# Layer 1's gate projection moved ahead of the attention loop and computed with seven half-size products

## The chip, the cores and the metric

One Trainium2 chip, one of its cores. The metric is device time in microseconds, median of several executions. TensorE is called PE, VectorE DVE, ScalarE ACT, GpSimd POOL, and SyncE SP; SP issues nearly all DMAs of this kernel, in order, from one queue.

## What is computed

Two layers over 640 tokens: 512 of a prompt and 8 x 16 of a sample group, 1024 features each. Layer 0 is a gated MLP with a spatial mixing per block of 128 tokens. Layer 1 is causal attention with 16 heads of 128 features and a learned forgetting bias; the sample group also reads 256 cached keys and values for each of its 8 rows. All is float32. The part that matters here, from the reference:

```
proj = h @ w_in
q, k, v = proj[..., :E], proj[..., E:2 * E], proj[..., 2 * E:3 * E]
z = proj[..., 3 * E:4 * E]
logf = log_sigmoid(proj[..., 4 * E:] + b_f)
...
op = (fox_attend_prompt(q, k, v, logf) * silu(z)) @ fox_w_out
```

h is 640 x 1024, and E is 2048, so that z is 640 x 2048. It meets the attention only at the very end, in a product element by element.

## The kernel before, in words

**Three products for one.** PE multiplies in a rounded float32 form. Each operand is kept as a high and a low part (`split`: ACT copies into the rounded form, DVE subtracts what was lost), and `mm3` (L249 to L251) issues three matmuls for each pair of operands.

**Weights.** `units` lists all weight panels in the order of use, 512 KB each. `fetch` issues the DMA of the next ones into three buffers `RAW`; `prefetch` splits them into the ring `W`, which has five slots of two halves (four in the attention part, where the fifth holds the split q and k of a head). `weights(n)` hands out the next n panels and asks `prefetch` to run ahead.

**Layer 0, seven products.** For u and z of each pair of 128-wide channel groups, `seven_products` (L523) does a 256 x 1024 by 1024 x 640 product as a 2 x 2 block product with seven half-size products in place of eight (Winograd's form of Strassen's scheme). A half-size product is 4 steps of 128 in depth, 128 channels by 320 tokens: 12 matmuls of 320 columns. It needs sums of weight blocks, which POOL makes for each pair (`left_operands`, L198, four operations), sums of blocks of h, which `right_operands` makes once (L400), and seven additions on DVE per pair to put the results together (L528, L538 to L543). z's end is a tanh on ACT (L582) and one operation on DVE (L583).

**Layer 1.** Heads go in eight pairs. `project_v`, `project_k`, `project_q` and `project_z` are generators that issue the matmuls of one pair with full depth, as `channel_steps` (L307) does for k, q and z: for a head 8 steps of 128 in depth, each with three matmuls of 384 and three of 256 columns, so 96 matmuls for a pair. `interleave` (L328) runs a generator and places pieces of other work between its steps, by a table of times. Lines 1090 to 1099 are the loop: first the projections of pair 0 alone, with the forgetting sums between them; then, for p = 0 to 6, the projections of pair p+1 with the attention of pair p in between, over a table of length 57 (p = 0 to 5: v, k, q and z) or 43 (p = 6: v, k and q alone). z of pair 7 runs after the loop, in `project_z(7)`. The attention of a pair is scores, softmax, transposes and values for two heads of the prompt (`prompt_pieces`) and two halves of the sample (`sample_pieces`); its cached keys come through one buffer in 8 DMAs of 128 KB (`load_k`, L974) with rows of 128 bytes, and are turned by DVE (`turn_k`, L992).

**Order.** A list scheduler sets the order of instructions on each engine's queue from the order of the code, the dependencies and its own model of time. The engines then run their queues in order.

Of the kernel before, what the change touches and what calls it, by code (L numbers as in the profile page):

```python
# [56 lines left out]
def hybrid_trunk(tc, x_prompt, x_sample, ck, cv, clf, p_prompt, p_sample, norm_pre, norm_post,  # L58
# [27 lines left out]
    c_sc = dram.tile([H, SEQ], F32, name="c_sc")  # L86
    cs_sc = dram.tile([P, 272], F32, name="cs_sc")
# [66 lines left out]
    for p in range(8):  # L154
        for part in (2, 1, 0, 3):
            for kk in range(2):
                u_rows(f_win[0], kk * 512, part * E + p * 256, 4, 256)
    u_tail(f_wout, 1)
# [3 lines left out]
    S0, S1 = 16, 48  # L162
    SEVEN = (0, 2)
    items = []
    for i in range(len(units)):
        if not S0 <= i < S1 or i % 4 - i % 2 not in SEVEN:
            items.append((i, None))
        elif i % 2 == 0:
            items += [(i, j) for j in range(4)]

    n0 = S1 + 16 + 2 + 8
    few = range(n0, n0 + 64 + 12)
    place, last_use = [], [-1] * (2 * NW)
    state = {"raw": 0, "used": 0}

    def raw_of(i):
        if S0 <= i < S1:
            z = (i - S0 + 1) % 4
            if z == NRAW:
                return r1(o_X, 1024)  # L180
        else:
            z = i % NRAW if i < S0 else (i + 1) % NRAW
        return RAW[:, z * 1024:z * 1024 + 1024]
# [7 lines left out]
    def left_operands(i, j):  # L191

        (a11, a21), (a12, a22) = ([raw_of(r).rearrange("p (k n) -> p k n", k=4)[:, :, z:z + P] for z in (0, P)] for r in (i, i + 1))
        s2, s3, s1, s4 = (SF[:, z * 512:z * 512 + 512].rearrange("p (k n) -> p k n", k=4) for z in range(4))
# [4 lines left out]
        return (a11, SF[:, :1024], SF[:, 1024:2048], raw_of(i + 1))[j]  # L199

    def prefetch(upto, i0=0):

        while len(place) < min(upto, len(items)):
# [15 lines left out]
            else:  # L219
                split(*((x.rearrange("p (k n) -> p k n", k=4) for x in (hi, lo)) if j == 0 else (hi, lo)), left_operands(u, j))  # L220
                if u > S0:
                    fetch(u + 4)
# [84 lines left out]
    def channel_steps(ws, hh, banks, splits=SPLITS):  # L307

        out = [bank(banks), bank(banks)]
        for k in range(8):  # L310
            w = [z[:, k % 4, hh * P:(hh + 1) * P] for z in ws[k // 4]]
            for (a, b), o in zip(splits, out):
                mm3(o[:, :b - a], w, h_at(k, a, b), k == 0, k == 7)
# [10 lines left out]

    def channel_unit(ws, hh, banks):
        return run(channel_steps(ws, hh, banks, ((0, TOK // 2), (TOK // 2, TOK))))
# [58 lines left out]
    o_X, o_ln, o_sum, o_th = 14208, 15232, 16256, 17216  # L385
# [4 lines left out]
    SF = pool2.tile([P, 2560], F32, name="sf")  # L390

# [6 lines left out]
    b11, b12, b21, b22, t_a, t_b = (r1(10240 + z * 1280, 1280).rearrange("p (k n) -> p k n", k=4) for z in (0, 1, 2, 3, 4, 0))  # L398

    def right_operands():  # L400

# [32 lines left out]
    for p in range(4):  # L434
# [4 lines left out]
        for kk in range(4):  # L439
# [5 lines left out]
            if (p, kk) == (1, 1):  # L445
                with queued("act", "dve"):
                    right_operands()
# [12 lines left out]
    fetch(S0 + 4)  # L460
# [25 lines left out]
    assert o_A + 256 <= o_X  # L486
# [31 lines left out]
    m1, u2, u3 = (r1(o_sum + z * HT, HT) for z in range(3))  # L518
    HALF = (slice(0, HT), slice(HT, TOK))

    UZ = (0, 1, 2, 3)

    def seven_products(into, done):  # L523

        rights = (quarter(0, 0), right_sum(1), quarter(0, 1), right_sum(0), quarter(1, 1), quarter(1, 0), right_sum(2))
# [24 lines left out]

    def eight_products(done):
        wz = weights(2)
        for i in range(2):
            for j, o in enumerate(channel_unit(wz, i, UZ)):
                done(i, j, o[:, :HT])
# [32 lines left out]
    for g in range(0, 16, 2):  # L588
        for part, finish in ((0, finish_u), (1, finish_z)):
            if 2 * part in SEVEN:  # L590
                seven_products(lambda i, j: uv_of(g + i)[part][:, HALF[j]], lambda i, j, c: finish(g, i, j, c))
            else:
# [552 lines left out]
```

## Time and profile before

| | us |
|---|---|
| median of 3 executions | 1334.62 (1334.31 to 1335.19) |
| profiled execution, its own time | 1334.83 |
| span of that execution | 1333.0 |
| PE busy | 1321.0 (99%) |
| DVE busy | 766.4 (57%) |
| ACT busy | 542.9 (41%) |
| POOL busy | 135.7 (10%) |

The time is that of the whole execution, the span reaches from the first to the last instruction of the program. Busy times of PE are a model of its pipeline: matmuls start before those ahead of them have ended, and the distance from one start to the next says what one of them costs. 172.87 MB go over the DMA queues in the span.

### The profile page before, as it was taken

How to read it: one execution, taken by the hardware profiler on the slowest of the kernel's cores; microseconds unless marked ns; L12 is line 12 of the kernel's file. 1: busy time of each engine (PE TensorE's matmuls, PEld its weight loads, DVE VectorE, ACT ScalarE, POOL GpSimd, SP SyncE). 2: the span in 40 equal slices, each digit the busy share in tenths (PEclk: the TensorE clock that was granted, in tenths of full speed). 3: DMA queues.
4: the chain of work that ended last, by engine and by line, in shares of the span. 5: the costliest groups of instructions: out<-in, count | busy, mean ns of one | idle time of the engine just before them, and what ended most of it. 6: DMA issues, size and time to landing. Idle time of an engine off the chain costs nothing.

```text
span 1333.0 us, 21550 instructions
## 1 busy us (share of the span) xinstructions
PE 1321.0 (99%) x8363; PEld 1191.6 (89%) x8363; DVE 766.4 (57%) x1581; ACT 542.9 (41%) x1025; POOL 135.7 (10%) x144
## 2 busy tenths in 40 slices
PE   9999999999999999999999999999999999999998
PEld 6888999999988788999999999999999998888786
DVE  7744899998844546544545454444545465544642
ACT  5434555444535334523433333433334344435341
POOL 1013444543000100000000000000000000000100
PEclk9999999999999999999999999999999999999999
DMA  6432334232324204688778575778778687243211
GB/s 224 138 100 70 120 114 130 66 109 68 127 95 158 78 18 127 178 142 158 138 154 176 145 163 141 164 144 163 125 151 169 152 212 235 101 149 111 64 64 47
DMA packets 299913, 172.87 MB, mean 130 GB/s; under 512 B 188769, under 2 KB 269201, under 8 KB 299810
## 3 DMA queue, kind: packets, MB, share of 16 engines
q1 hardware_dynamic: 299666, 171.23, 51.7%
q8 instruction: 65, 1.06, 0.3%
q14 instruction: 38, 0.31, 0.1%
q10 hardware_dynamic: 144, 0.26, 0.1%
HBM read 149.86 MB, written 21.59 MB: 129 GB/s over the span
## 4 chain that ended last, share of the span: by engine, by line
PE 94%; DVE 3%; issue 1%; ACT 1%; DMA 0%; POOL 0%; SPq 0%; DVEq 0%
PE pb L249 28%; PE pb L251 27%; PE pb L250 27%; PE pb L960 3%; PE pb L953 1%; PE pb L1014 1%; PE pb L1040 1%; PE pb L287 1%; DVE W L264 1%; PE pb L565 1%; PE pb L1037 1%; DVE R L583 0%; DMA RAW<-in_gmlp_w_in 0%; PE pb L1032 0%; DVE R L528 0%
## 5 line engine op out<-in xcount | busy, mean ns | idle before, releaser
L249 PE MATMUL pb<-A,W 128*128 128x384 f32 (+2 forms) x1024 | 330.2, 322 | 2.1 <-DVE R L538 1.8
L251 PE MATMUL pb<-A,W 128*128 128x384 f32 (+2 forms) x1024 | 317.1, 310 | 0.0
L250 PE MATMUL pb<-A,W 128*128 128x384 f32 (+2 forms) x1024 | 316.6, 309 | 0.0
L249 PE MATMUL pb<-W,A 128*128 128x512 f32 (+1 forms) x840 | 298.3, 355 | 2.1 <-ACT R L686 1.4
L251 PE MATMUL pb<-W,A 128*128 128x512 f32 (+1 forms) x840 | 293.7, 351 | 0.6 <-DVE A L264 0.6
L250 PE MATMUL pb<-W,A 128*128 128x512 f32 (+1 forms) x840 | 294.0, 350 | 0.0
L264 DVE TENSOR_TENSOR W<-RAW,W 128x1024 fp32r<-128x1024 f32 (+1 forms) x156 | 194.0, 1244 | 139.7 <-ACT W L263 137.5
L263 ACT ACTIVATE W<-RAW 128x1024 fp32r<-128x1024 f32 (+1 forms) x156 | 161.1, 1033 | 156.8 <-PE pb L250 65.1
L249 PEld LDWEIGHTS pb<-A,W 128*128 128x128 f32 x1024 | 193.0, 188 | 10.9 <-issue 6.8
L250 PEld LDWEIGHTS pb<-A,W 128*128 128x128 f32 x1024 | 193.0, 189 | 0.6
L251 PEld LDWEIGHTS pb<-A,W 128*128 128x128 f32 x1024 | 192.6, 188 | 0.4 <-issue 0.4
L249 PEld LDWEIGHTS pb<-W,A 128*128 128x128 f32 x840 | 159.1, 189 | 26.4 <-issue 3.1
L251 PEld LDWEIGHTS pb<-W,A 128*128 128x128 f32 x840 | 158.9, 189 | 21.1 <-DVE A L264 0.9
L250 PEld LDWEIGHTS pb<-W,A 128*128 128x128 f32 x840 | 159.0, 189 | 20.4 <-issue 0.4
L264 DVE TENSOR_TENSOR A<-R,A 128x640 fp32r<-128x640 f32 (+1 forms) x51 | 41.0, 835 | 74.1 <-ACT A L263 71.9
L992 DVE STREAM_TRANSPOSE r2b_t<-r2b_t 128x256 f32<-128x256 f32 x128 | 46.4, 413 | 33.9 <-PE pb L1014 26.2
L263 ACT ACTIVATE A<-R 128x640 fp32r<-128x640 f32 (+1 forms) x51 | 36.6, 746 | 67.7 <-PE pb L250 65.7
L249 PE MATMUL pb<-tb,W 128*128 128x320 f32 x192 | 59.8, 312 | 0.1
L251 PE MATMUL pb<-tb,W 128*128 128x320 f32 x192 | 59.5, 310 | 0.0
L250 PE MATMUL pb<-tb,W 128*128 128x320 f32 x192 | 59.5, 310 | 0.0
L273 POOL TENSOR_TENSOR SML<-SML 128x1 f32<-128x1 f32 x25 | 18.1, 724 | 385.1 <-DVE SML L271 380.5
L955 ACT ACTIVATE R<-pb 128x128 f32<-128x128 f32 (+1 forms) x64 | 27.9, 436 | 65.7 <-PE pb L953 65.4
(235 smaller groups left out, 1866.7 us busy)
## 6 DMA issues: line engine op xcount, KB each, us to landing
RAW<-in_fox_w_in SPq DMA_DIRECT2D x64, 512.0 KB
RAW<-in_gmlp_w_in SPq DMA_DIRECT2D x40, 512.0 KB
r2b_t<-in_cache_fox_v SPq DMA_DIRECT2D x32, 512.0 KB
r2b_t<-in_cache_fox_k SPq DMA_DIRECT2D x128, 128.0 KB
RAW<-in_gmlp_w_out SPq DMA_DIRECT2D x16, 512.0 KB
RAW<-in_ple_w_gate SPq DMA_DIRECT2D x16, 512.0 KB
RAW<-in_fox_w_out SPq DMA_DIRECT2D x16, 512.0 KB
out<-R SPq DMA_DIRECT2D x40, 128.0 KB
```

Of the source, the lines that this page charges most:

```text
L249: nc.tensor.matmul(out, lh, rh, start=start, stop=False)
L250: nc.tensor.matmul(out, lh, rl, start=False, stop=False)
L251: nc.tensor.matmul(out, ll, rh, start=False, stop=stop)
L263: nc.scalar.activation(out=hi, in_=src, func=AF.Copy)
L264: nc.vector.tensor_tensor(out=lo, in0=src, in1=f(hi), op=ALU.subtract)
L273: nc.gpsimd.tensor_tensor(out=q, in0=t, in1=mhalf, op=ALU.pow)
L287: nc.tensor.transpose(out=b[:, j * P:(j + 1) * P], in_=src[:, (4 * c + j) * P:(4 * c + j + 1) * P], identity=ident)
L565: nc.tensor.matmul(b0[:, t * P:(t + 1) * P], v_at(pnl, t)[:, c0:c0 + P], wm, start=True, stop=True)
L953: nc.tensor.transpose(out=tb[:, j * P:(j + 1) * P], in_=pr[:, j * P:(j + 1) * P], identity=ident)
L955: nc.scalar.activation(out=pt[:, :n], in_=tb[:, :n], func=AF.Copy)
L960: nc.tensor.matmul(O[:, d], v[:, j, hh * P:(hh + 1) * P], pt[:, j * P:(j + 1) * P], start=(j == 0), stop=(j == i))
L992: nc.vector.transpose(out=kt[:, hh, bl, :PAST], in_=kr[:, hh, bl])
```

## The change

z of pairs 0 to 6 is taken out of the projections of the loop. A stage of its own, between k of pair 0 and q of pair 0, computes it pair after pair with `seven_products`, and writes it to a DRAM tensor `z_sc` (640 KB a pair). In the loop, `z_again` reads it back at the start of each pair's attention. The order of the weight panels follows. All of p = 0 to 6 now use the table of length 43; p = 0 has later times for its sample pieces, since its cached keys are loaded at the loop's start. z of pair 7 stays where it was, after the loop.

What goes with it: `right_operands` is called a second time, for layer 1's h, and gives four sums (before, the fourth overwrote a quarter of h). The second large pool of SBUF holds these sums during the stage, and becomes the attention's buffers after it; the small tensors of the forgetting bias move to the first pool. POOL's four sums for each pair go to a part of that pool too, and `RAW` has a fourth slot in the stage.

The diff, cut to its core:

```
+    z_sc = dram.tile([H, P, TOK], F32, name="z_sc")
...
-    for p in range(8):
-        for part in (2, 1, 0, 3):
+    def u_pair(p, parts):
+        for part in parts:
             for kk in range(2):
                 u_rows(f_win[0], kk * 512, part * E + p * 256, 4, 256)
+
+    u_pair(0, (2, 1))
+    Z0 = len(units)
+    for p in range(7):
+        u_pair(p, (3,))
+    Z1 = len(units)
+    u_pair(0, (0,))
+    for p in range(1, 8):
+        u_pair(p, (2, 1, 0) if p < 7 else (2, 1, 0, 3))
...
+    SEVEN = ((16, 48, 14208), (Z0, Z1, 13504))
...
-    few = range(n0, n0 + 64 + 12)
+    few = range(Z1, n1 + 12)
...
-        for o, a, b, dst in ((t_a, b12, b11, 0), (t_b, b22, t_a, 1), (b21, b21, t_b, 2), (b12, b22, b12, None)):
+        for o, a, b, dst in ((b11, b12, b11, 0), (b12, b22, b12, t3), (b22, b22, b11, 1), (b21, b21, b22, 2)):
             nc.vector.tensor_tensor(out=o, in0=a, in1=b, op=ALU.subtract)
             if dst is not None:
                 split(*right_sum(dst), o)
+        return b12
...
-    pool2, R2 = second("r2b", F32)
+    pool2, TB = second("r2k", F32R)
+    state["sums"] = r1(10496, 2048)
...
+    def make_z(p):
+
+        zst = r1((7456, 15168)[p % 2], 2 * TOK)
+
+        def into(i, j):
+            return zst[:, i * TOK:(i + 1) * TOK][:, HALF[j]]
+
+        def done(i, j, c):
+            th = r1(14528 + j * HT, HT)
+            nc.scalar.activation(out=th, in_=c, func=AF.Tanh, scale=0.5)
+            nc.vector.scalar_tensor_tensor(out=into(i, j), in0=th, scalar=1.0, in1=c, op0=ALU.add, op1=ALU.mult)
+
+        seven_products(into, done, right_sum(3), 12544)
+        dma(z_sc[2 * p:2 * p + 2].rearrange("h p t -> p h t"), zst.rearrange("p (h t) -> p h t", h=2))
+
+    def z_again(p):
+        dma(r1(RA + (p % 2) * 4608 + 3328, 2 * TOK).rearrange("p (h t) -> p h t", h=2), z_sc[2 * p:2 * p + 2].rearrange("h p t -> p h t"))
...
-    PARTS = (project_v, project_k, project_q, project_z)
-    interleave(project(0, PARTS), [(0.0, forget_logits), (6.0, log_forget), (20.0, forget_sums), (30.0, lambda: load_k(0, 0))])
+    PARTS = (project_v, project_k, project_q)
+    interleave(project(0, PARTS[:2]), [(8.0, lambda: right_operands(12544, 3)), (16.0, forget_logits), (23.0, log_forget)])
     for p in range(7):
-        length, step = (57, 5.6) if p < 6 else (43, 4.2)
-        pieces = kv_times(p, 0, 5) + kv_times(p, 1, length / 2) + sample_times(p, 0, 5) + sample_times(p, 1, length / 2)
-        pieces += [(2, lambda p=p: load_k(p, 1)), (length / 2 - 3, lambda p=p: load_k(p + 1, 0))]
+        make_z(p)
+        if p == 1:
+            forget_sums()
+    pool2.release()
+    pool2, R2 = second("r2b", F32)
+    run(project_q(0))
+    length, step = 43, 4.2
+    for p in range(7):
+
+        t0, t1 = (12, 27) if p == 0 else (5, length / 2)
+        pieces = [(t0 - 14, lambda p=p: z_again(p))]
+        if p == 0:
+            pieces.append((0, lambda: load_k(0, 0)))
+        pieces += kv_times(p, 0, t0) + kv_times(p, 1, t1) + sample_times(p, 0, t0) + sample_times(p, 1, t1)
+        pieces += [(t0 - 3, lambda p=p: load_k(p, 1)), (t1 - 3, lambda p=p: load_k(p + 1, 0))]
         for hh in range(2):
             pieces += prompt_times(2 * p + hh, 2 + 4 * step * hh, step)
-        interleave(project(p + 1, PARTS if p < 6 else PARTS[:3]), pieces)
+        interleave(project(p + 1, PARTS), pieces)
         store_y(p)
```

How instructions move, at three places. In these rows R_69 is the large first pool of SBUF, r2k_t the tile of the right sums, pb_70 to pb_77 are the banks of PSUM, A holds h, W the split weights, and a shape is that of the output.

First DVE, from the last splits of h to the first results of the new stage. Before, this stretch held weight splits and the small operations of the forgetting bias:

```order
L264 TENSOR_TENSOR A<-pb_75,A 128x4x128
L264 TENSOR_TENSOR W<-RAW,W 128x1024
L781 COPY r2b_t<-pb_76 128x160
L782 TENSOR_TENSOR r2b_t<-r2b_t 128x80
...
L867 COPY R_69<-pb_72 128x128
L869 STREAM_TRANSPOSE R_69<-R_69 128x512
```

And now:

```order
L279 TENSOR_TENSOR A<-pb_75,A 128x4x128
L417 TENSOR_TENSOR R_69<-A 128x1280 x2
L419 TENSOR_TENSOR R_69<-R_69 128x1280 x2
L279 TENSOR_TENSOR W<-R_69,W 128x1024
L419 TENSOR_TENSOR R_69<-R_69 128x1280
L279 TENSOR_TENSOR r2k_t<-R_69,r2k_t 128x1280
L279 TENSOR_TENSOR W<-R_69,W 128x1024
L419 TENSOR_TENSOR R_69<-R_69 128x1280
L279 TENSOR_TENSOR r2k_t<-R_69,r2k_t 128x1280 x2
L873 COPY R_69<-pb_72 128x128
L787 COPY R_69<-pb_76 128x160
L279 TENSOR_TENSOR r2k_t<-R_69,r2k_t 128x1280
```

The sums of h's blocks (L417, L419) and their splits into r2k_t stand between the last split of h and the first copy of k (L867 before, L873 now); the forgetting bias (L781 before, L787 now) comes after them.

Second PE, at the end of a pass of the loop. Before, at the end of p = 3, z of the next pair stands last ahead of v of the pair after it:

```order
L960 MATMUL pb_77<-R_69 128x128 x4
L249 MATMUL pb_73<-A,W 128x384
...
L249 MATMUL pb_70<-A,W 128x256
...
L249 MATMUL pb_71<-W,A 128x256
...
L931 MATMUL pb_76<-R_69 128x128
```

And now, at the end of p = 0:

```order
L264 MATMUL pb_71<-A,W 128x384
...
L264 MATMUL pb_72<-A,W 128x256
...
L984 MATMUL pb_77<-R_69 128x128 x4
L1071 MATMUL pb_75<-CST,R_69 128x128 x2
L264 MATMUL pb_73<-W,A 128x256
...
L955 MATMUL pb_76<-R_69 128x128
```

The last projection ahead of the next pass is now q of the very pair whose scores (L931 before, L955 now) follow after 18 matmuls of v.

Third SP, from the last weights of the new stage to the first loads of the loop, now:

```order
L121 DMA z_sc<-R_69 128x2x640
L121 DMA RAW<-in_fox_w_in 128x4x256 x2
L121 DMA r2b_t<-c_sc 128x512
L121 DMA r2b_t<-in_cache_fox_k 32x32x32 x6
...
L121 DMA r2b_t<-in_cache_fox_k 32x32x32 x2
...
L121 DMA r2b_t<-in_cache_fox_v 128x4x256 x2
L121 DMA RAW<-in_fox_w_in 128x4x256
```

The loads into r2b_t (forgetting sums, cached keys) wait until the stage's last product has read r2k_t, whose place they take; the weights of pair 1's v and k stand ahead of them, those of its q behind the first of them.

## Rows read from the trace of the kernel before

**Rows 1.** The page, part 1: busy time, share of the span and instructions of each engine.
```profile
PE 1321.0 (99%) x8363; PEld 1191.6 (89%) x8363; DVE 766.4 (57%) x1581; ACT 542.9 (41%) x1025; POOL 135.7 (10%) x144
```
**Rows 2.** The page, part 4: the chain that ended last, by engine.
```profile
PE 94%; DVE 3%; issue 1%; ACT 1%; DMA 0%; POOL 0%; SPq 0%; DVEq 0%
```
**Rows 3.** Timeline of PE (start, duration): z of pair 0 begins; v of pair 1 begins.
```profile
592.09 0.34 PE L249 MATMUL pb<-A,W 128*128 128x384 f32 x1
...
606.27 0.29 PE L249 MATMUL pb<-W,A 128*128 128x256 f32 x1
```
**Rows 4.** Timeline of PE: starts of v of pairs 2, 6, 7, and of z of pair 7.
```profile
680.15 0.29 PE L249 MATMUL pb<-W,A 128*128 128x256 f32 x1
...
975.70 0.29 PE L249 MATMUL pb<-W,A 128*128 128x256 f32 x1
...
1049.59 0.29 PE L249 MATMUL pb<-W,A 128*128 128x256 f32 x1
...
1109.15 0.42 PE L249 MATMUL pb<-A,W 128*128 128x384 f32 x1
```
**Rows 5.** Busy time by stretch: passes p = 0, 5 and 6 of the loop.
```profile
core 0: us, PE busy (x) PEld busy (x) DVE busy (x) ACT busy (x) POOL busy (x), PEclk, DMA share, GB/s
606.30:680.20 73.90, 73.90 (x571) 70.27 (x570) 36.04 (x110) 27.39 (x62) 1.51 (x6) 1.00 0.80 158
...
975.70:1049.60 73.90, 73.90 (x571) 70.27 (x570) 36.04 (x110) 27.20 (x62) 1.39 (x6) 1.00 0.72 152
1049.60:1109.20 59.60, 59.60 (x475) 55.92 (x473) 32.50 (x104) 25.02 (x57) 2.15 (x6) 1.00 0.82 193
```
**Rows 6.** Timeline of PE: layer 0's first z, seven products, and the instruction after.
```profile
139.62 0.31 PE L249 MATMUL pb<-A,W 128*128 128x320 f32 x1
...
151.93 0.38 PE L565 MATMUL pb<-R 128*128 128x128 f32 x2
```
**Rows 7.** Busy time by stretch (columns as in rows 5): layer 0's sixteen seven-product parts.
```profile
126.90:347.50 220.60, 218.35 (x1518) 216.58 (x1517) 201.90 (x308) 114.79 (x211) 91.90 (x58) 1.00 0.33 101
```
**Rows 8.** Groups in that stretch: count, busy us, mean ns, idle before and releaser.
```profile
L249 PE MATMUL pb<-A,W 128*128 128x320 f32 x256 | 80.8, 316 | 2.1 <-DVE R L538 1.8 <-ACT R L536 0.3
L264 DVE TENSOR_TENSOR W<-sf,W 128x1024 fp32r<-128x1024 f32 x30 | 36.7, 1222 | 5.4 <-ACT W L263 5.4
L264 DVE TENSOR_TENSOR W<-RAW,W 128x1024 fp32r<-128x1024 f32 (+1 forms) x26 | 35.5, 1369 | 1.7 <-ACT W L263 1.7
...
L528 DVE TENSOR_TENSOR R<-R,pb 128x320 f32<-128x320 f32 x63 | 29.0, 477 | 0.4
L198 POOL TENSOR_TENSOR sf<-RAW,sf 128x512 f32<-128x512 f32 x14 | 28.7, 2051 | 1.1
...
L583 DVE SCALAR_TENSOR_TENSOR R<-sf,R 128x320 f32<-128x320 f32 x15 | 17.1, 1137 | 1.0
...
L198 POOL TENSOR_TENSOR sf<-R,RAW 128x512 f32<-128x512 f32 x7 | 9.1, 1300 | 19.8 <-DVE W L264 19.8
L583 DVE SCALAR_TENSOR_TENSOR R<-R 128x320 f32<-128x320 f32 x14 | 7.9, 566 | 0.8
...
L264 DVE TENSOR_TENSOR W<-R,W 128x512 fp32r<-128x512 f32 x7 | 5.7, 812 | 0.3 <-ACT W L263 0.3
```
**Rows 9.** Timeline of PE: the first matmul after the last transposes of h.
```profile
550.70 0.36 PE L249 MATMUL pb<-W,A 128*128 128x256 f32 x1
```
**Rows 10.** Layer 0's block sums of h, L406 (ns, min/median/max), and their splits.
```profile
L406 DVE TENSOR_TENSOR R<-R x4: 1481/1482/1483, 53.3 to 60.1; 128x1280 f32<-128x1280 f32 x4
...
L264 DVE TENSOR_TENSOR tb<-R,tb 128x1280 fp32r<-128x1280 f32 x3 | 4.4, 1482 | 0.0
...
L263 ACT ACTIVATE tb<-R 128x1280 fp32r<-128x1280 f32 x1 | 1.3, 1277 | 2.0 <-DVE R L406 2.0
```
**Rows 11.** DMA over the passes p = 5 and p = 6: packets and bytes.
```profile
DMA packets 29936, 11.27 MB, mean 152 GB/s; under 512 B 22368, under 2 KB 29416, under 8 KB 29928
...
DMA packets 28903, 11.51 MB, mean 193 GB/s; under 512 B 22420, under 2 KB 27228, under 8 KB 28897
```

More of the change, by code (lines that the diff above doesn't have):

```diff
@@ L153, in hybrid_trunk @@
     u_tail(g_wout, 0)
-    for p in range(8):
-        for part in (2, 1, 0, 3):
+    def u_pair(p, parts):
+        for part in parts:
             for kk in range(2):
                 u_rows(f_win[0], kk * 512, part * E + p * 256, 4, 256)
+    u_pair(0, (2, 1))
[6 more added lines that the diff above has]
+        u_pair(p, (2, 1, 0) if p < 7 else (2, 1, 0, 3))
+    n1 = len(units)
     u_tail(f_wout, 1)
-    S0, S1 = 16, 48
-    SEVEN = (0, 2)
+    SEVEN = ((16, 48, 14208), (Z0, Z1, 13504))
     items = []
+    raw_slot, raw_last = [], [-1] * (NRAW + 1)
+    part_of = {}
     for i in range(len(units)):
-        if not S0 <= i < S1 or i % 4 - i % 2 not in SEVEN:
+        part = next((x for x in SEVEN if x[0] <= i < x[1]), None)
+        if part is None:
             items.append((i, None))
-        elif i % 2 == 0:
+        elif i % 2 == part[0] % 2:
             items += [(i, j) for j in range(4)]
-    n0 = S1 + 16 + 2 + 8
-    few = range(n0, n0 + 64 + 12)
+            part_of[i] = part
+        if part and i == part[0]:
+            raw_last[NRAW] = i
+        z = min(range(NRAW + (part is not None)), key=lambda z: raw_last[z])
+        raw_last[z] = i
+        raw_slot.append(RAW[:, z * 1024:z * 1024 + 1024] if z < NRAW else r1(part[2], 1024))
+    few = range(Z1, n1 + 12)
     place, last_use = [], [-1] * (2 * NW)
-    state = {"raw": 0, "used": 0}
+    state = {"raw": 0, "used": 0, "sums": None}
     def raw_of(i):
[L177 to L183, printed above, removed]
+        return raw_slot[i]
     def fetch(upto):
@@ L193, in left_operands @@
         (a11, a21), (a12, a22) = ([raw_of(r).rearrange("p (k n) -> p k n", k=4)[:, :, z:z + P] for z in (0, P)] for r in (i, i + 1))
-        s2, s3, s1, s4 = (SF[:, z * 512:z * 512 + 512].rearrange("p (k n) -> p k n", k=4) for z in range(4))
+        sf = state["sums"]
+        s2, s3, s1, s4 = (sf[:, z * 512:z * 512 + 512].rearrange("p (k n) -> p k n", k=4) for z in range(4))
         if j == 0:
@@ L305, in hybrid_trunk, with channel_steps @@
     SPLITS = ((0, SA), (SA, TOK))
-    def channel_steps(ws, hh, banks, splits=SPLITS):
+    def channel_steps(ws, hh, banks):
         out = [bank(banks), bank(banks)]
@@ L311, in channel_steps @@
             w = [z[:, k % 4, hh * P:(hh + 1) * P] for z in ws[k // 4]]
-            for (a, b), o in zip(splits, out):
+            for (a, b), o in zip(SPLITS, out):
                 mm3(o[:, :b - a], w, h_at(k, a, b), k == 0, k == 7)
@@ L390, in hybrid_trunk @@
     SF = pool2.tile([P, 2560], F32, name="sf")
+    state["sums"] = SF[:, :2048]
     def quarter(i, j):
@@ L459, in hybrid_trunk @@
         load_ln(0)
[L460 removed]
+    fetch(20)
     mu, rs, shift = [], [], []
```

38 lines of the change are left out of this document (14 added, 24 removed).

## The prediction

> **What bounds the kernel now.** Busy times come first: PE is busy 99% of the span, DVE 57%, ACT 41% [rows 1]. That alone doesn't say that PE is the bound, since an average hides stages; the chain of waits does: 94% of the chain that ended last is PE's own work, and nothing else has more than 3% [rows 2]. Then the stages that the change touches. In the loop of layer 1 PE is busy for the whole of every pass, at a granted clock of 1.00, with DVE at 36.0 of 73.9 us and the DMA engines at 0.72 to 0.80 [rows 5]. In the stretch of layer 0 that already uses seven products PE is idle for 2.25 of 220.6 us, and there DVE is close behind at 201.9 us [rows 7]. So time goes away only where PE's work goes away, and DVE and the DMA engines are the two that could take its place. Since matmuls overlap, I take what PE's work costs from the distance between starts, never from busy times.
>
> **What the change removes.** z of pair 0 runs with nothing between its matmuls from 592.09 to 606.27: 14.18 us for 96 matmuls, 0.148 each [rows 3]. z of pairs 1 to 6 stands in the passes p = 0 to 5. From v of pair 1 at 606.27 to v of pair 7 at 1049.59 these take 443.3 us, 73.9 each [rows 3, 4]. What a pass takes without z needs no model, since p = 6 is one: it has the table of length 43, the same attention, and v, k and q alone. It runs from 1049.59 to 1109.15, 59.56 us [rows 4], with PE busy throughout [rows 5]. Six such passes take 357.4 us, so the loop loses 86.0. Some of it is not matmuls: without z there are fewer places where PE goes from attention work back to a projection. Removed in all: 100.1 us.
>
> **What it adds on PE.** A seven-product z takes 12.31 us in layer 0 (139.62 to 151.93, with no pause between its 84 matmuls [rows 6]). Its shapes are those of layer 1: 128 channels by 320 tokens, four steps of depth. Seven of them: 86.2 us. All else on PE stays, the forgetting logits and sums too; the attention pieces of a pass now stand in the order that p = 6 had. Sum of PE's work: 86.2 - 100.1 = **-14.0 us**. This is the gain if nothing waits.
>
> **What it adds elsewhere, and what hides it.**
> - *The sums of h's blocks*, at the start. After the last transposes (550.70 [rows 9]) PE has, by the new order, 154 matmuls until the second product of the first z, the first that reads such a sum. At 0.148 each, a little less since more of them are 256 wide, that is about 22 us. DVE has in that time: the last two splits of h (1.2, an estimate: half of a 1024-wide split each), six sums of 1.48, three splits of 1.48 [rows 10] and two weight splits of 1.22 [rows 8]: 17.0 us. It makes it with 5 us in hand. If ACT's copy (1.28) stood bare ahead of each of the three splits, it would be 20.8, still in time; if POOL's four sums of 1.3 to 2.1 us [rows 8] held DVE up as well, 27, 5 late. Bounds 0 and 5; I take 1. k's copies and transposes queue behind these on DVE and then have their own 8 DMAs per head on SP; nothing on PE waits for those.
> - *DVE in the stage.* Per z: four weight splits (77.9 us for 63, so 4 x 1.24 = 4.95), seven additions of 0.48 (3.34), and the four last operations at 1.137 and 0.566 (2 of each, 3.41) [rows 8]. That is 11.7 of 12.31 us, 95%, against 91.5% in layer 0's stretch [rows 7]. It fits, but with little room, and for seven z in a row without the spatial work that fills PE in layer 0. There PE lost 1.8 us to DVE in sixteen parts [rows 8], so seven parts lose 0.8 at the same rate. Bounds 0 and the rival below; I take 1.5.
> - *POOL* needs four sums per z, 5.2 to 8.2 us by its shortest and longest mean [rows 8]. ACT does four copies, one m1 and four tanh, less than DVE. Both fit in 12.31.
> - *DMA in the stage:* 1.05 MB of weights in and 0.66 MB of z out per 12.3 us, 139 GB/s; p = 6 moved 193 GB/s with PE busy throughout [rows 5].
> - *DMA in the loop:* a pass of the old kind moved 11.27 MB. Without z's weights and with z read back it is 10.9 MB, in 59.6 us; p = 6 moved 11.51 MB in that time [rows 11]. z's read stands at the start of a pass on SP's queue and is needed at its end. I cost it at nothing.
> - *The first pass.* The first loads of the attention's buffers wait until the stage's last product has read r2k_t, and SP is held there. The weights of pair 1's v and k are issued ahead of them; q of pair 0 and the first matmuls of v follow on PE, some 16 us for a 256 KB load. Bounds 0 and 3, taken from the longest case in which the scores of the first pass start one row of the table late (4.2 steps); I take 0.5.
>
> **Sum.** -14.0 + 1 + 1.5 + 0.5 = -11.0 us on the profiled execution's 1334.83, so 1323.8. That execution is 0.2 above the median of the runs shown, so the forecast for the median is **1323.6 us**.
>
> **Rivals.**
> 1. *DVE and POOL exclude each other (slower).* The last operation on z takes 1.137 us in one form and 0.566 in the other, and POOL's sums 2.05 or 1.30 [rows 8]: something makes both wait. If two-input operations of DVE and POOL's sums never overlapped, a z would need 4.95 + 4 x 0.566 + 4 x 1.30 = 12.4 us, and with the 3.34 of additions in the same queue 15.8. Seven times 3.5 more is +24, so +10 against before: about 1346. It decides from 14.3 us per z on (12.31 + 14.0 / 7). Against it: in layer 0 DVE and POOL were busy 201.9 and 91.9 us of 220.6 [rows 7], so they overlapped for at least 73 us, though a part of that may be waiting. The Trainium skill (SBUF — State Buffer, Who interferes with whom) states such a rule: a DVE instruction with two SBUF inputs contends with a GpSimd instruction that reads SBUF, and the one that comes second is blocked fully. By that rule the additions, which read one input from PSUM, can run beside POOL, and a z needs 12.4 us, a loss of 0.7 us in the stage in place of the 1.5. The long and the short form agree with the rule; how far POOL's work is idle waiting no row tells. Chance 0.06.
> 2. *The DMA engines bound the shorter passes (slower).* p = 0 kept them busy 0.80 of 73.9 us, 59 us [rows 5]. If a pass went on needing that at a share of 0.82, the most that any pass had, it would last 72 us and nothing would be won in the loop: 12.5 x 6 = +75, far slower. It decides from 2.3 us per pass on. Against it: p = 6 moved as many packets and more bytes in 48.9 us of busy time (0.82 x 59.6) [rows 5, 11]. For it: p = 6 was a single one, six in a row could pile up. Chance 0.04.
> 3. *Half of the gain is lost in small waits.* q of a pair now ends just ahead of its own pass, so that its last copies stand between it and the scores, where z stood before; p = 6 doesn't show this. At 0.7 us per pass that is 4 us, with 4 more at the stage's start: 1326 to 1332. Against it: the first scores come after 18 matmuls of v, some 2 us. Chance 0.17.
> 4. *The change doesn't pay:* the stage takes 14 us per z, for DVE's lag, and gives back what it saves. 1332 to 1337. Chance 0.05.
>
> **How the numbers follow.** The forecast (1320.5 to 1326) has 0.68. 0.2% of 1334.6 is 2.7 us, about what a measurement of this kernel can tell from no change. Faster by more than that, under 1331.9, are the forecast and rival 3: 0.85. The same is rival 4: 0.05. Slower are rivals 1 and 2: 0.10. The range 1320 to 1331.5 goes from the bare sum on PE (1334.6 - 14.0 = 1320.6) with little below it, since no row shows PE doing more than this, to the far end of rival 3, and holds some 0.83.
>
> **What would show it.** In the changed kernel: z's 84 matmuls in 12.3 us from first to last, seven times in a row, with under 0.5 us of idle PE per z; passes of 59.6 us (starts of v to starts of v); DVE at 0.95 of the stage. A gap on PE ahead of the first product that reads r2k_t would be the first loss, gaps with DVE as their releaser inside the stage the second. Wrong I'd be if a z took over 14 us, if passes took over 62, or if PE waited for a DMA in the loop.

## The result, and the profile after

The changed kernel takes 1338.09 us (median; 1334.27 to 1340.86) against 1334.59 (1334.23 to 1336.05) of the kernel before: a ratio of 1.0024, interval 1.0017 to 1.0030. It is slower, by a little over 0.2%. The forecast was 1323.6. The times of the changed kernel also lie over three times as far apart as those of the kernel before (6.6 us against 1.8).

The busy times and the chain that ended last, of the changed kernel (its profiled execution took 1336.04 us, span 1333.9):

```profile
PE 1311.2 (98%) x8279; PEld 1180.8 (89%) x8279; DVE 834.3 (63%) x1656; ACT 562.6 (42%) x1050; POOL 178.0 (13%) x172
...
PE 87%; DVE 6%; DMA 4%; issue 1%; ACT 1%; SPq 1%; POOL 1%; DVEq 0%; ACTq 0%; POOLq 0%
```

PE is busy 9.8 us less than in [rows 1], yet the span is longer; its part of the chain fell from 94% [rows 2] to 87%, and DMA, next to nothing before, has 4%. Where these stand, the busy times by stretch show: the first, second and fourth z of the stage (the third begins at 612.43), and the passes p = 0, 1, 2.

```profile
core 0: us, PE busy (x) PEld busy (x) DVE busy (x) ACT busy (x) POOL busy (x), PEclk, DMA share, GB/s
576.28:594.62 18.34, 14.60 (x88) 14.17 (x87) 15.11 (x28) 9.52 (x14) 3.40 (x2) 0.91 0.61 108
594.62:609.68 15.06, 12.95 (x86) 12.23 (x84) 9.49 (x18) 5.10 (x8) 7.25 (x6) 1.00 0.59 138
...
624.83:637.15 12.32, 12.32 (x87) 12.32 (x86) 11.47 (x16) 5.58 (x9) 5.86 (x5) 1.00 0.52 137
688.40:750.80 62.40, 60.19 (x474) 56.05 (x473) 33.52 (x106) 24.70 (x57) 1.18 (x5) 1.00 0.89 173
750.80:812.40 61.60, 60.38 (x476) 56.41 (x474) 32.70 (x106) 22.57 (x55) 1.34 (x6) 1.00 0.84 176
812.40:872.00 59.60, 59.60 (x474) 55.92 (x474) 32.42 (x104) 24.52 (x56) 2.15 (x6) 1.00 0.99 197
```

A z in the steady stage takes 12.32 us with PE busy throughout, and a pass from p = 2 on 59.65: both within 0.1 us of the forecast. The loss stands in two places. First, the start of the stage. PE's timeline gives the first matmul of v of pair 0 and of pair 1, here of the changed kernel:

```profile
538.39 0.28 PE L264 MATMUL pb<-W,A 128*128 128x256 f32 x1
...
688.40 0.28 PE L264 MATMUL pb<-W,A 128*128 128x256 f32 x1
```

and here the first of them in the kernel before (the second is in [rows 3], at 606.27):

```profile
538.70 0.28 PE L249 MATMUL pb<-W,A 128*128 128x256 f32 x1
```

The distance was 67.57. Less z of pair 0 (14.18), plus seven z of 12.31, it should be 139.6. It is 150.01: **10.4 us lost**. Second, the passes p = 0 and 1, 2.8 and 1.9 us over 59.65: **4.7 us lost**. The tally of this execution: from v of pair 0 to v of pair 7 the kernel before takes 510.9 us (538.70 to 1049.59 [rows 4]). With nothing lost it would now be 139.6 and six passes of 59.65, 497.5, which is 13.4 less. With 10.4 and 4.7 lost it is 1.7 more, and so it is measured (538.39 to 1050.95). The rest of the program took 0.8 less in this execution, for which no run gives a cause; that makes the 0.9 us by which the span is longer.

What PE waits for at the start, by its waits from 538 to 612 (sum, times, longest):

```profile
PE pb L264 <- ACT R L550: 5.2, 2, 3.7
...
PE pb L777 <- DVE WF L279: 2.2, 1, 2.2
```

L550 is ACT's copy of the first product of a z (m1), which frees a bank that PE needs. L777 is the first matmul of the forgetting bias. PE is idle for 8.1 us in all. And the idle time has a price behind it: after the longest wait the granted clock is 0.52, near the lower of the two levels (1.2 of 2.4 GHz). PE by timeline, and the clock of that stretch:

```profile
core 0: us, PE busy (x) PEld busy (x) DVE busy (x) ACT busy (x) POOL busy (x), PEclk, DMA share, GB/s
...
586.00:589.00 3.00, 3.00 (x12) 3.00 (x13) 3.00 (x6) 2.95 (x4) 0.22 (x1) 0.52 0.45 66
```

```profile
585.93 0.47 PE L264 MATMUL pb<-A,W 128*128 128x320 f32 x1 [3.74 <-ACT R L550]
586.20 0.47 PE L265 MATMUL pb<-A,W 128*128 128x320 f32 x1
...
589.78 0.31 PE L266 MATMUL pb<-r2k_t,W 128*128 128x320 f32 x1
```

From 585.93 to 589.40 the starts lie 0.267 apart instead of 0.147: 13 of them, 1.6 us more. Idle time and low clock make 9.7 of the 10.4.

Why m1 is late is in ACT's timeline: a weight split stands ahead of it and waits for a panel from DRAM.

```profile
584.92 0.63 ACT L278 ACTIVATE W<-R 128x512 fp32r<-128x512 f32 x1 [7.19 <-DMA R<-in_fox_w_in]
585.46 0.42 ACT L550 ACTIVATE R<-pb 128x320 f32<-128x320 f32 x1
```

The chain of waits from 540 to 612 goes further back. Its pieces (start, duration):

```profile
554.23 3.27 DMA R<-in_cache_fox_logf
...
557.74 1.20 DVE A L279 x2
558.94 2.80 DVE R L417 x2
...
567.21 2.51 DVE r2k_t L279
569.71 1.14 DVE W L279
...
570.93 2.49 POOL R L213
...
573.49 2.43 POOL R L213
...
575.93 0.37 SPq L121
...
576.39 8.42 DMA R<-in_fox_w_in
...
584.92 0.64 ACT W L278
...
590.23 7.92 DMA RAW<-in_fox_w_in
...
598.28 1.31 POOL R L213
...
601.00 1.07 ACT W L278
```

Read from the top: DVE's copy of the cached forget logits (L760) waits for a small load; behind it in DVE's queue stand the last splits of h and the sums of its blocks; beside these POOL makes the left sums of pair 1; only when POOL has read its panels are their places free, and SP, held there since 565, issues the next load; it takes 8.4 us to land, and ACT's split, ahead of m1, waits for it. Between 580 and 590 SP issues the 16 transfers of k, and the next panel behind them goes out at 590.23; POOL, then a split, then the second z's m1 wait for that.

In the loop's first pass (chain from 674 to 720) the same thing happens once more, with a panel that stood behind the key loads on SP's queue, so that ACT's split waits for it for 6.0 us:

```profile
703.02 8.81 DMA RAW<-in_fox_w_in
711.85 1.06 ACT W L278
712.94 1.23 DVE W L279
```

### The profile page after: what moved, and what is told of

Its sections match the earlier page's. It is cut to its first block, busy times and chain, and to the rows that moved or that the text cites. A ratio compares the mean times of both kernels' runs of the same rounds, so it can differ in the third digit from the quotient of the medians.

```text
span 1333.9 us, 21602 instructions
## 1 busy us (share of the span) xinstructions
PE 1311.2 (98%) x8279; PEld 1180.8 (89%) x8279; DVE 834.3 (63%) x1656; ACT 562.6 (42%) x1050; POOL 178.0 (13%) x172
## 3 DMA queue, kind: packets, MB, share of 16 engines
q8 instruction: 65, 1.06, 0.3%
## 4 chain that ended last, share of the span: by engine, by line
PE 87%; DVE 6%; DMA 4%; issue 1%; ACT 1%; SPq 1%; POOL 1%; DVEq 0%; ACTq 0%; POOLq 0%
PE pb L264 26%; PE pb L266 25%; PE pb L265 25%; PE pb L984 3%; DMA RAW<-in_fox_w_in 2%; DVE W L279 2%; PE pb L302 1%; PE pb L977 1%; PE pb L1064 1%; PE pb L1038 1%; PE pb L573 1%; DMA R<-in_fox_w_in 1%; DVE R L591 1%; SPq L121 1%; POOL R L213 1%
## 5 line engine op out<-in xcount | busy, mean ns | idle before, releaser
L264 PE MATMUL pb<-A,W 128*128 128x384 f32 (+2 forms) x884 | 284.5, 322 | 7.9 <-ACT R L550 5.4
L266 PE MATMUL pb<-A,W 128*128 128x384 f32 (+2 forms) x884 | 274.0, 310 | 0.0
L265 PE MATMUL pb<-A,W 128*128 128x384 f32 (+2 forms) x884 | 273.6, 309 | 0.0
L278 ACT ACTIVATE W<-RAW 128x1024 fp32r<-128x1024 f32 (+1 forms) x154 | 156.7, 1018 | 142.4 <-PE pb L266 53.8
L264 PEld LDWEIGHTS pb<-A,W 128*128 128x128 f32 x884 | 166.6, 188 | 17.9 <-issue 6.8
L265 PEld LDWEIGHTS pb<-A,W 128*128 128x128 f32 x884 | 166.6, 188 | 0.7
L266 PEld LDWEIGHTS pb<-A,W 128*128 128x128 f32 x884 | 166.3, 188 | 0.4 <-issue 0.4
L279 DVE TENSOR_TENSOR W<-R,W 128x512 fp32r<-128x512 f32 (+1 forms) x56 | 48.1, 870 | 11.2 <-ACT W L278 11.2
```

The costliest lines, as they stand in the source:

```text
L264: nc.tensor.matmul(out, lh, rh, start=start, stop=False)
L265: nc.tensor.matmul(out, lh, rl, start=False, stop=False)
L266: nc.tensor.matmul(out, ll, rh, start=False, stop=stop)
L278: nc.scalar.activation(out=hi, in_=src, func=AF.Copy)
L279: nc.vector.tensor_tensor(out=lo, in0=src, in1=f(hi), op=ALU.subtract)
```

## The experiments

The theory: PE's saving is real, but panels and small loads land late, and ACT's and DVE's queues, which go in order, then stand behind a wait with the short copies that PE needs. The rivals: DVE and POOL hold each other up; ACT's table loads for the forget gates are what is late; the DMA engines lack time. "Start" is from v of pair 0 to v of pair 1 in the profiled execution (139.6 expected), p0 and p1 the first two passes (59.65 expected), and the ratio is to the kernel before (median 1334.78 over 25 executions beside these). Each kernel of the table has 4 to 12 executions.

| kernel | median us | ratio, interval | start | p0 | p1 |
|---|---|---|---|---|---|
| changed, again | 1338.15 | 1.0025, 1.0016 to 1.0034 | 150.14 | 60.77 | 63.19 |
| A: fourth panel buffer elsewhere | 1339.39 | 1.0033, 1.0020 to 1.0045 | 151.15 | 62.03 | 64.20 |
| B: small loads back | 1332.21 | 0.9980, 0.9971 to 0.9989 | 144.73 | 61.99 | 62.37 |
| C: forget gates later | 1339.13 | 1.0037, 1.0025 to 1.0050 | 151.30 | 63.81 | 60.99 |
| D: B + own tanh scratch | 1329.13 | 0.9963, 0.9953 to 0.9973 | 142.45 | 62.03 | 62.82 |
| E: B + second keys six units later | 1332.29 | 0.9979, 0.9971 to 0.9988 | 142.69 | 64.39 | 60.51 |
| F: D + E + C | 1331.46 | 0.9970, 0.9960 to 0.9981 | 141.93 | 64.93 | 60.78 |
| G: B, pair 1's POOL sums left out | 1327.62 | 0.9951, 0.9939 to 0.9962 | 140.27 | 62.03 | 61.85 |
| H: D, one key load left out | 1323.91 | 0.9917, 0.9903 to 0.9930 | 142.34 | 59.71 | 59.63 |
| I: D + first keys in the stage | 1324.47 | 0.9917, 0.9903 to 0.9930 | 142.51 | 59.71 | 59.64 |
| K: I + C | 1325.32 | 0.9921, 0.9908 to 0.9935 | 142.64 | 59.70 | 59.63 |
| L: tanh scratch alone | 1340.52 | 1.0045, 1.0033 to 1.0058 | 150.11 | 63.57 | 63.63 |
| M: first keys in the stage alone | 1333.55 | 0.9987, 0.9978 to 0.9996 | 150.07 | 59.71 | 59.63 |
| N: D, z's reload left out | 1330.99 | 0.9970, 0.9959 to 0.9981 | 142.05 | 60.34 | 63.36 |
| I again | 1324.17 | 0.9919, 0.9905 to 0.9933 | 142.89 | 59.71 | 59.63 |
| O: I without the tanh scratch | 1327.19 | 0.9936, 0.9924 to 0.9948 | 144.77 | 59.71 | 59.63 |

**The changed kernel again.**

> The changed kernel again, beside the others of this series. Every theory expects 1334 to 1341 us, the spread of the runs already shown; in the profile V of pair 1 starts about 150 us after V of pair 0, and the seven passes take 62.4, 61.6 and five times 59.65 us. If the first two passes or the start of the stage differ by over 2 us between two executions of one kernel while the steady z's do not, what is lost there hangs on the time at which transfers land and not on a fixed amount of engine work.

The start is the same to 0.1 us, though the longest wait lies elsewhere (2.85 us at 603 here, 3.74 at 586 there). The two passes lose 4.7 us together in both executions, divided otherwise (1.1 and 3.5 here, 2.8 and 1.9 there). No part differs by the 2 us that were to decide, so this run leaves the cause open; it shows that the place of a wait changes from one execution to the next.

**A, the fourth panel buffer.**

```
-    SEVEN = ((16, 48, 14208), (Z0, Z1, 13504))
+    SEVEN = ((16, 48, 14208), (Z0, Z1, 9216))
...
-    nc.gpsimd.memset(r1(RA + 9216, 1024), 0.0)
...
+    nc.gpsimd.memset(r1(RA + 9216, 1024), 0.0)
     run(project_q(0))
```

> The fourth buffer of raw weights lies no longer over the scratch in which the right operands' sums are made, so that no load has to wait for those sums. Theory (late weight panels behind which ScalarE's queue stands): the load that was held 11.2 us at the head of the transfer queue goes out at once, the 3.7 us idle of TensorE near 586 us disappears and the start of the stage is 3 to 5 us shorter, 1333 to 1335 us. Rival that VectorE and GpSimd, sharing SBUF, are what is late there: under 1 us, 1337 to 1338 us. Rival that the activation table loads of the forget gates are what is late: under 1 us as well.

The first half of the expectation came, the second did not. The panel of the fourth buffer goes out at 542.91, and the 3.7 us idle near 586 are gone. But SP is still held until 576.27, by another panel whose place POOL's sums must free; the one after that still goes out behind k's transfers, and the second z now waits 5.29 us in one piece, at 602.69. The chain of this kernel there:

```profile
588.29 1.47 SPq L121
589.86 7.75 DMA RAW<-in_fox_w_in
597.74 1.27 POOL R L213
599.08 1.27 POOL R L213
```

Taking one link out of a chain of late loads moved the wait to the next link. Behind that wait PE runs 17 matmuls at some 0.27 us instead of 0.147, and the start is 1 us longer than before.

**B, the small loads.** Their buffers lie in a part of R1 that layer 0's last part does not use.

```
-    wf_raw = tmpa(128).rearrange("p (k n) -> p k n", k=8)
+    wf_raw = r1(16896, 128).rearrange("p (k n) -> p k n", k=8)
...
-    cc = tmpa(256).rearrange("p (t b h) -> p t b h", t=2, b=NB)
+    cc = r1(17024, 256).rearrange("p (t b h) -> p t b h", t=2, b=NB)
```

> The two small loads of layer 1's start (forget weights and cached forget logits) go back to buffers that are free before layer 0's last part, so that they need not wait for it. Theory (late loads hold up the queues in order): ScalarE's 4.9 us wait and VectorE's 4.0 us wait at the head of the first K and V products disappear, h's block sums are done 3 to 4 us earlier and the stage starts 2 to 4 us sooner, 1334 to 1336 us. Rival that the sums are limited by VectorE and GpSimd excluding each other: the sums end at the same time give or take 1 us and the time stays at 1337 to 1338 us.

5.9 us, more than the 2 to 4 expected. The wait at L777 is gone, and the panel that stood behind the 16 transfers of k went out at 578.91, ahead of 12 of them, instead of 590.23; PE is idle for 3.0 us at the start instead of 8.1. The expectation also had the sums of h's blocks end 3 to 4 us earlier. They ended 1.1 us earlier (40.2 us after v of pair 0 begins, instead of 41.4): on that point the rival of DVE and POOL was the better forecast, and G takes it up. A wait of ACT's that remains, and the longest of PE's:

```profile
ACT L902 <- DMA out<-R: 2.6, 1, 2.6
...
PE pb L264 <- DVE R L542: 2.1, 1, 2.1
```

The tanh (L902) writes its scratch to the place of k's staging tile and waits until k has left it; DVE's operation behind it (L903) and then L542 are late by that.

**C, forget gates later.**

```
-    interleave(project(0, PARTS[:2]), [(8.0, lambda: right_operands(12544, 3)), (16.0, forget_logits), (23.0, log_forget)])
+    interleave(project(0, PARTS[:2]), [(8.0, lambda: right_operands(12544, 3)), (16.0, forget_logits)])
     for p in range(7):
         make_z(p)
         if p == 1:
+            log_forget()
+        if p == 2:
             forget_sums()
```

> The logarithm of the forget gates (with its three activation table loads) stands after the second z of the stage in place of ahead of the first, the forget sums after the third. Theory (late weight panels): the idle time at the first z only shrinks where the table loads stand between a late split and TensorE's copies, 1 to 2 us, 1336 to 1337 us. Rival that the table loads are what holds TensorE at the start: 4 to 5 us of the 10.4 lost there come back, 1333 to 1334 us. Moved into the steady part of the stage they can cost there what they save, then the time stays at 1338 us.

Nothing is won alone, nor on top of others (F, K). In K the second z, from its first matmul to that of the third, takes 12.71 us instead of the 16.96 of I, but the third then takes 17.05 instead of 12.41 (the forgetting sums, in the second before and in the third now, are a part of that): the price moves with the operations. So moving them is no remedy. That the table loads cost something wherever they stand is not excluded.

**D, L and O, the tanh scratch.**

```
-            th = r1(14528 + j * HT, HT)
+            th = r1((3328 if p == 0 else 14528) + j * HT, HT)
```

> On top of the small loads moved back (that kernel took 1332.2 us), the tanh scratch of pair 0's z no longer shares its place with the staging tile of k, so that ScalarE's first tanh need not wait until k's transfers to the output have left. Theory (ScalarE and VectorE stand in order behind something that waits for a transfer): the 2.6 us wait for that transfer and the 2.1 us idle of TensorE at 593 us go, 1 to 2 us less, 1330 to 1331.5 us. Rival that the table loads in front of this tanh are what is late: the wait is only renamed, 1332 us as before.

> The changed kernel with the tanh scratch of pair 0's z moved away from k's staging tile, and nothing else. If the two losses add up: 2 to 3 us under the changed kernel's 1338.1, 1335 to 1336.5 us. If the late small loads hide this wait (the tanh comes after k's transfers anyhow, since TensorE is held up longer before it): no difference, 1337 to 1339 us.

> The version with small loads moved back, a tanh scratch of its own and early keys again, beside the next one: 1324.5 us, start of the stage 142.5 us, first passes 59.7.

> The same without the edit of the tanh scratch. If k's transfers hold the first tanh and with it TensorE: 2 to 3 us more, 1326.5 to 1327.5 us, and a wait of ScalarE's tanh for a transfer to the output of 2 us or more. If the table load and the split behind it are what TensorE waits for: within 1 us of the other, 1324 to 1325.5 us.

With the small loads in time it gives about 3 us (D against B; I again against O, run side by side, 1324.17 and 1327.19). On the changed kernel as it is it gives nothing (L is 2.4 us slower, its passes 63.6 each): there the first tanh comes later, at 590.68, and does not wait for k's transfers. O shows the wait, 2.8 us:

```profile
589.85 1.28 ACT L902 ACT_TABLE_LOAD   x1 [2.78 <-DMA out<-R]
```

In I the same instruction starts at 584.80 and waits for nothing. Its share of the start can't be given closely, since B and E, with the same code up to there and the same wait of PE for L542 (2.13 and 2.12 us), differ by 2 us in the start (144.73 and 142.69). Most of this is the clock: after its wait B ran at the lower level for 3 us, and E did not.

```profile
594.00:597.00 3.00, 3.00 (x13) 3.00 (x13) 3.00 (x5) 2.69 (x5) 1.28 (x1) 0.50 0.81 212
```

```profile
594.00:600.00 6.00, 5.70 (x39) 5.70 (x40) 5.90 (x12) 3.62 (x6) 1.47 (x1) 1.00 0.93 270
```

(B above, E below, columns as before.) In the profiled executions PE's idle time is only 0.7 us shorter in D than in B, and 0.5 to 0.8 in the two of I than in O.

**E, the first pass's second key loads six units later,** meant to stand behind the panel.

```
-        pieces += [(t0 - 3, lambda p=p: load_k(p, 1)), (t1 - 3, lambda p=p: load_k(p + 1, 0))]
+        pieces += [(t0 + (3 if p == 0 else -3), lambda p=p: load_k(p, 1)), (t1 - 3, lambda p=p: load_k(p + 1, 0))]
```

> On top of the small loads moved back (1332.2 us), the key loads of the first pass's second half are issued six units later, behind the weight panel instead of ahead of it. Theory (a weight panel queued behind key loads lets ScalarE wait 5 to 6 us, with TensorE's copies behind it): the first two passes, 62.0 and 62.4 us, lose 1 to 3 us together, 1329.5 to 1331.5 us. Rival that the transfers themselves are what the shorter passes lack: the wait moves to the key transposes or the second pass, and the time stays at 1332 us or rises by up to 2 us.

p0 and p1 together take 124.9 us against 124.4 in B. But the edit hardly changed SP's order: one of the eight key loads, and not all, now stands behind the panel, which goes out 14.3 us after v of pair 1 begins instead of 15.4. B, then E, then M, in which the first keys go out in the stage:

```profile
697.64 1.31 SPq L121 DMA_DIRECT2D RAW<-in_fox_w_in  x2
```

```profile
696.28 0.51 SPq L121 DMA_DIRECT2D RAW<-in_fox_w_in  x1
```

```profile
696.03 0.42 SPq L121 DMA_DIRECT2D RAW<-in_fox_w_in  x1
```

In M this is the panel after that one, 7.8 us after v of pair 1 begins; the one before it is out 0.7 us ahead of v. So E does not decide whether the order on the queue costs anything.

> Small loads moved back, tanh scratch of its own, key loads later, the forget gates' logarithm after the second z and their sums after the third, all together. Theory: the stage's start loses 1 to 3 us instead of 10.4, the first passes 2 to 4 instead of 5, 1327 to 1330 us. If what is late is the sum of all work in front of TensorE at the start and not the order of the queues, no better than the small loads alone, 1332 us.

F, all of these together, gains nothing over D (1331.5 and 1329.1): the edits of E and C bring nothing there either.

**G, POOL's sums of pair 1 left out.**

```
-        if j == 0:
+        if j == 0 and not i == Z0 + 2:
```

> On top of the small loads moved back (1332.2 us), the four GpSimd sums of pair 1's left operands are left out (that z is made from the sums of pair 0). Rival (VectorE's sums and differences of h's blocks are long because GpSimd works on SBUF beside them): the differences of 1280 columns, 1.40 to 2.6 us beside GpSimd, all take 1.4 us, the start of the stage is 2 to 4 us shorter, 1328.5 to 1330.5 us. Theory (late transfers): only the wait for a raw panel that GpSimd's sums keep goes, 0 to 1.5 us, 1331 to 1332.5 us.

The rival holds part of the truth. DVE's timeline in B, with POOL's sums beside it:

```profile
568.92 2.47 POOL L213 TENSOR_TENSOR R<-RAW 128x512 f32<-128x512 f32 x1 [2.57 <-DVE W L279]
571.47 2.43 POOL L213 TENSOR_TENSOR R<-R,RAW 128x512 f32<-128x512 f32 x1
...
570.17 2.58 DVE L419 TENSOR_TENSOR R<-R 128x1280 f32<-128x1280 f32 x1
572.66 2.58 DVE L279 TENSOR_TENSOR r2k_t<-R,r2k_t 128x1280 fp32r<-128x1280 f32 x1
```

and in G, where POOL has nothing to do then:

```profile
570.48 1.49 DVE L419 TENSOR_TENSOR R<-R 128x1280 f32<-128x1280 f32 x1
571.88 1.48 DVE L279 TENSOR_TENSOR r2k_t<-R,r2k_t 128x1280 fp32r<-128x1280 f32 x1
```

The sums of h's blocks end 36.6 us after v of pair 0 begins, 40.2 in B, and the start loses 0.7 us, the least of all runs, though the first tanh still waits 2.3 us for k's transfers there: with DVE ahead, that wait costs PE 0.6 us at most. G also lets SP go sooner (it waits 7.8 us for POOL from 540 to 612, 10.8 in B), and its clock falls less, so its 4.6 us under B are an upper bound for what this contention costs. No run leaves the sums out of the changed kernel as it is.

**H, I and M, the first passes' loads.** In H the second key load of pair 0 is left out:

```
         pieces += [(t0 - 3, lambda p=p: load_k(p, 1)), (t1 - 3, lambda p=p: load_k(p + 1, 0))]
+        if p == 0:
+            del pieces[-2]
```

In I and M the first is issued beside z of pair 5:

```
-        kr = r2(o_K, 2048).rearrange("p (h b n) -> p h b n", h=2, b=4)
+        kr = (r1(5408, 2048) if i == 0 else r2(o_K, 2048)).rearrange("p (h b n) -> p h b n", h=2, b=4)
...
-        return [(t0 - 2, lambda: load_v(p, bg)), (t0 - 4, lambda: turn_k(p, bg))]
+        return [(t0 - 2, lambda: load_v(p, bg)), (t0 - 4 if p or bg else 2, lambda: turn_k(p, bg))]
...
+        if p == 5:
+            load_k(0, 0)
...
-        if p == 0:
-            pieces.append((0, lambda: load_k(0, 0)))
```

> On top of the version with small loads moved back and a tanh scratch of its own (1329.1 us): the past keys of pair 0's second half of the samples are not loaded in the first pass (1 MB in 8 transfers; the keys of the first half are used in their place). The first two passes there take 62.0 and 62.8 us against 59.65 each of the others. Theory A (the first passes lack transfer time: the DMA engines are over 90 percent busy from the loop's start on): both come near 59.65, 4 to 5 us less in all, 1324.5 to 1326 us. Theory B (it is the order in ScalarE's queue behind one late panel, whatever the amount): the first pass gains at most 1 to 2 us and the second stays, 1327.5 to 1329 us.

> On top of the same version (1329.1 us): the first key load of pair 0 goes out in the stage, beside the z of pair 5, into a part of R1 that is free there, and not at the loop's start. Theory A (first passes lack transfer time): the 1 MB moved out of the first pass gives 2 to 4 us, 1325 to 1327 us. Theory B (order of the queue): 0 to 1.5 us, 1327.5 to 1329 us. If the stage, which moves its panels at the same time, has no transfer time to spare, its steady 12.32 us per z grow by 1 us or more and nothing is gained.

> The changed kernel with the first key load of pair 0 moved into the stage and nothing else. If the loss in the first two passes is one of its own (they lack transfer time): these take 59.7 us each and 4 to 5 us go, 1333 to 1334.5 us; the start of the stage keeps its 150 us. If it came from the late start: passes of 62 us as before and 1337 to 1339 us.

All three make both passes run at 59.7 us, and I costs the stage nothing (12.32 us per z as before). M gives 4.6 us alone, I 4.7 on top of D: this loss is one of its own, and the key loads that fall into the first pass are its cause.

> The version with early keys, and besides the logarithm of the forget gates after the second z and their sums after the third. Theory (table loads in ScalarE's queue hold the first tanh by what is left there, 1.6 us idle of TensorE at 593 us): 0.5 to 1.5 us less than the version with early keys. Rival (the wait only moves to the z after it, as when it was done alone): the same within 0.5 us.

K is no better than I.

**N, z's reload left out** for pairs 0 and 1:

```
-        pieces = [(t0 - 14, lambda p=p: z_again(p))]
+        pieces = [(t0 - 14, lambda p=p: z_again(p))] if p > 1 else []
```

> On top of the version with small loads moved back and a tanh scratch of its own (1329.1 us, first passes 62.0 and 62.8 us): the reloads of z of pairs 0 and 1 from DRAM are left out (2 transfers of 640 KB; stale numbers stand in their place). If it is the bytes that count, 0.64 MB out of each of the two passes gives two thirds of what the 1 MB of keys gave, 3 us, 1326 us. If it is the 8 transfers of small pieces that count (128 KB each of 128 byte pieces), z's reload in long pieces costs little, 0 to 1.5 us, 1327.5 to 1329 us.

Nothing is won in the time (the two passes together take 123.7 us, 124.9 in D), so z's way through DRAM is not what the first passes lack time for. Packets and bytes from 667 to 745 us, in D:

```profile
DMA packets 43750, 13.67 MB, mean 175 GB/s; under 512 B 36021, under 2 KB 42848, under 8 KB 43744
```

in N:

```profile
DMA packets 43661, 13.11 MB, mean 168 GB/s; under 512 B 36101, under 2 KB 43015, under 8 KB 43655
```

and in I:

```profile
DMA packets 38461, 13.43 MB, mean 172 GB/s; under 512 B 30253, under 2 KB 37559, under 8 KB 38455
```

N moves fewer bytes than I and still loses; what I has less of is small packets, and issues on SP's queue (24 key transfers instead of 32). And a third thing goes with these two: in every kernel that loses here, the panel stands behind seven or eight key loads and goes out 12.7 to 15.8 us after v of pair 1 begins, in H at 2.7 and in I and M ahead of v. Which of the three it is, the engines' time for small packets, SP's time to issue them, or the panel's place on the queue, no run separates.

## Why the prediction was wrong

- *PE's work, -14.0.* Right within 0.6 us. A z takes 12.32 us against 12.31, later passes 59.65 against 59.56, which makes -13.4. With the three mended places (I) 2.9 us are lost at the start and none in the loop: -10.5, where the forecast has -11.0, and its 1324.5 and 1324.2 us lie within 1 us of the forecast 1323.6. That it comes so close is in part luck: the start lost 2.9 where 1 was taken, and DVE in the stage some 0.1 where 1.5 was.
- *DVE in the stage, 1.5.* Smaller: from the third z on PE lost nothing to speak of, with DVE busy 11.5 of 12.3 us.
- *"k's copies and transposes ... nothing on PE waits for those": the step that failed at the start*, with the sums of h's blocks (bounds 0 and 5, 1 taken). In place of the 1 that these terms were given, the start lost 10.4. The working counted how long DVE needs and found 5 us in hand; it did not ask what stands in front of DVE's and ACT's queues, nor what SP must issue behind k's transfers. k's transfers stood ahead of a panel that a z needed (chain and A), and their staging tile is where the tanh writes (O). And the move of the forgetting bias's small tensors into the first pool was not priced at all: their loads then wait for layer 0's last part, and their place alone is worth 5.9 us (B).
- *POOL beside DVE.* The working gave DVE 17.0 us there, and 27 "if POOL's four sums ... held DVE up as well". The same operations took 19.6 in the changed kernel, from the last splits of h (557.66) to the third split of a sum (577.25), and 22.1 with the fourth split (579.76); the four splits of 1280 columns took 2.15 to 2.59 each instead of 1.48. They also began only at 557.66, behind the small loads. Beside POOL's sums of 2.4 (1.30 alone) a DVE operation of 1.48 took 2.58, so that a pair needs nearly the sum of both. In B's rows above the two engines end in turn (POOL 571.39, DVE 572.75, POOL 573.90, DVE 575.24), each about its own time alone after the other. The Trainium skill (SBUF — State Buffer, Who interferes with whom) states that a DVE instruction with two SBUF inputs contends with a GpSimd instruction that reads SBUF; the trace agrees, with the figures just given. Rival 1 put this into the steady stage, where PE stayed busy all the same; it bit where DVE had a backlog.
- *The first pass, 0.5 (bounds 0 and 3), and DMA in the loop, nothing.* Mis-sized: 2.8 in p = 0 and 1.9 in p = 1. The key loads that had their place in the part ahead of the loop can only start once the stage has freed the second pool, and fall on top of the first pass's own; the working costed the wait for the first of them, and not what stands behind them. The DMA engines' share from 690 to 710 us, in the changed kernel and in M (columns as before):

```profile
690.00:710.00 20.00, 20.00 (x166) 19.09 (x165) 9.99 (x34) 5.03 (x13) 0.47 (x2) 1.00 1.08 221
```

```profile
690.00:710.00 20.00, 20.00 (x167) 19.10 (x165) 11.61 (x40) 7.79 (x19) 0.47 (x2) 1.00 0.88 235
```

  From 674 to 690 it is 0.96 in the changed kernel, and 1.06 in M, which loses nothing: a high share is not by itself the loss. Rival 2 (passes of 72 us) fits two passes of seven at most, at about a fifth of its price; that it is the engines' time, and not the queue, is not shown. From p = 2 on it was wrong: a share of 0.99 and PE busy throughout.
- *Rivals 3 and 4.* Rival 3's copies ahead of the scores cost 0.1 us a pass from p = 2 on, and not 0.7. Rival 4 named nearly the time that came, by a mechanism that did not: a z takes 12.32 us and not 14.
- *The spread.* Some executions lose 0.4 to 3.5 us in the sixth pass too: in M's profile it took 63.10, ACT's splits having waited for panels for 9.8 us. And a part lies ahead of all that was changed here: v of pair 0 begins at 537.24 in I and at 540.92 in I again, 3.7 us of the 4.1 between these two executions. The 2 us between the changed kernel's profiled run and its median are not explained by a trace; either would do it, and that is only argued.
- *What stays open:* the rest of 2.9 us at the start in I (PE idle for 2.3, the longest 1.55 with DVE's L542 as releaser), and the share of the contention in it, which G's 0.7 us lost lets seem large; and what in the first pass's key loads it is that costs 4.7 us.

## What to carry to other kernels

When a stage moves, price its small loads and the places of its scratch tiles like its large operations: list, for each engine's queue at the new seam, what the instruction in front waits for and which load can only go out once a tile is free. Queues that go in order turn one late panel into a wait of everything behind it, and mending a single link can then show no gain: the wait moved to the next link in A, and the tanh scratch gave nothing in L and 3 us once the small loads were mended (D). And price a loop's first pass by the loads that pile up in it and by what stands behind them on the queue, not by the mean of a steady pass. After an edit that is meant to change an order, read the order from the trace before drawing a conclusion (E).

## What the runs showed that was not expected

- A PE idle for 3.74 us came back at a granted clock of 0.52 and ran 13 matmuls at 0.267 us each instead of 0.147: 1.6 us on top of the wait. After a wait of 2.1 us the clock fell in B and stayed at 1.00 in E.
- Leaving out the reloads of z for two pairs, 1.3 MB in pieces of 2.5 KB gave nothing (N), while moving 1 MB of 128 byte pieces elsewhere gave 4.6 us (M).
- Steady passes of the loop keep PE fully busy with the DMA engines at 0.99 of a pass (p = 2), so a high share alone does not mark a bound.
